# Four edits of order in a two-layer hybrid backbone: GLA's first projections, its scores and states, its gate products, and two adaLN k tiles

## The chip, the core and the metric

One core of a Trainium2 chip runs the whole program in one launch. The metric is device microseconds of that core, the median of several runs. TensorE (PE) multiplies, VectorE (DVE) and ScalarE (ACT) do elementwise work and empty PSUM, GpSimd (POOL) does a few small operations, SyncE (SP) issues every DMA.

## The reference, cut to what matters

Two layers work on 256 latent and 256 context tokens of width 1024. Each layer is: an adaLN-modulated RMS norm, one input projection, three token mixers, gated merging, an output projection with a gated residual, a second modulated norm, and a squared-ReLU MLP with a gated residual.

```python
sh1, sc1, ga1, sh2, sc2, ga2 = split(c_silu @ mod_w + mod_b, 6)        # per layer; the same for the context
h = rms_norm(x) * (1 + sc1) + sh1
y1 = rglru_branch(...)      # two directions: a*h + u scans over tokens, times gelu(y)
y2 = gla_branch(...)        # 4 heads, 2 directions: chunked gated linear attention, RMS norm, silu(r) gate
y3 = gqa_branch(...)        # 8 query heads, 2 key/value heads, softmax
x = x + ga1 * (merge of y1, y2, y3 by sigmoid gates) @ w_out
x = x + ga2 * squared_relu_mlp(rms_norm(x) * (1 + sc2) + sh2)
```

In GLA, with b the running sum of the log gates in a chunk of 64 tokens, a direction computes `scores = (q exp(b - b_mid)) (k exp(b_mid - b))^T`, masked, and a state `s` that decays by `exp(b_last)` from chunk to chunk and takes up `(k exp(b_last - b))^T v`. The output is `scores v + (q exp(b)) s`, summed over both directions.

## The kernel before, in words

Activations lie transposed: features on the partitions, the 512 tokens (context first, then latent) along the free axis. Layer 0 computes all tokens, layer 1 only the latent ones where the context isn't needed any more.

**Gemms.** `weight` (lines 191 to 202) loads a 512 KB tile of weights on SP's queue, casts it on ACT to a high part `wh` (L200) and subtracts on DVE for the low part `wl` (L201). `gemm` (line 252) makes 24 matmuls for 128 output features, `hi*hi`, `hi*lo` and `lo*hi` for each of eight k tiles, into one of the four PSUM banks of the pool `mm`. `gemm_tok` (line 265) does it token by token for four token tiles at once and wants four such banks. The other four banks are the pool `mx`. All matmuls of both helpers have the line L212.

**Order.** The program is traced as straight code. A scheduler then orders each engine's queue by priority, which is the place in the trace; `tc.high_priority(n)` moves a block n places ahead. It takes a lower instruction where the higher ones aren't ready, by its own estimate of time. The chip then runs each engine's queue in that order. Tiles come from pools with a fixed number of slots: `t2` has ten (`tmp()`), `g2` three (`gtmp()`), `t1` fifteen (`tmp1()`).

**RG-LRU and the passage to GLA.** Lines 605 to 622 go through eight channel tiles in pairs: convolution, gates on PE and ACT, decay, a square root (L614), then `lru_scan` (L529 to L540), ten DVE instructions and one cast on ACT (L282) for a tile. Behind the last pair's scans stand `gla_gates(0)`, the log gates of GLA's head 0 (Abs L585, Exp L588, Ln L589 on ACT; L586, L592 and two scans L594, L596 on DVE). Then `gla(0)` begins with the key and query gemms, copied out of PSUM on ACT by L637 and L640, and the value `gemm_tok`, copied by L645.

**A GLA head** (`gla`, line 632). For each direction: exponentials, scores on PE (L699, L701), a masked copy (L705), a turn of the decayed keys (L712) into `kt` (L715, L717, L718; from `t2`), and at once the three state products (L725) with their updates (L728, L730). Then the outputs (L744), their RMS norm (L746 to L751), and for each half j: the gate gemm, its silu (L755, L756; `y` from `t2`), the turn of the output (L759), their product and its split into two parts. Behind head 1 and head 2 stand four merges each (`merge`, line 767): two gemms, a tanh (L771) into a tile of `g2`, and a product into `m`.

**adaLN columns.** `mods` (line 310) is a task that is interleaved with the gemms by a clock of its own, which counts matmul columns: `tick` steps it when the clock has passed its next time. For each half of a unit (1024 columns) it loads eight k tiles of 256 KB. ACT makes the first product with the conditioning vector (L339) and DVE adds the others (L341), for two vectors. It pauses `pace` after each k tile and `M_S` at the end. `mod_cols` (line 288) then sums over the partitions on PE, by a matmul of each sum with a column of ones in `pick` (32 columns, one for each of four groups of PSUM partitions), and turns the row into columns of `modT` (L308). The turn of a half is traced behind the sum of the next one. Layer 0's second norm needs units 3 and 4: `need(l, 3, 4)` (line 953) steps the task until they are done.

Of the kernel before, what the change touches and what calls it, by code (L numbers as in the profile page):

```python
# [18 lines left out]
AF = mybir.ActivationFunctionType  # L19
# [4 lines left out]
KT = 8  # L24
# [13 lines left out]
GZP, G0P = 2, 6  # L38
AHEAD = 800
L_SM, L_PT = 4.0, 1.5  # L40
M_A, M_K, M_S = 300, 3.0, 2.0
NDVE = (0, 2, 5)
NL = 2
O_LX, O_LY, O_GQ, O_GK, O_GV, O_GR, O_GZ = 0, 1024, 2048, 2560, 3072, 4096, 5120
# [60 lines left out]
def trunk_kernel(ctx: ExitStack, tc: tile.TileContext, out: bass.AP, d: dict):  # L105
# [17 lines left out]
    def tmp():  # L123
        return t2.tile([128, 512], F32, name="t2")
# [163 lines left out]
    def mod_cols(l, n, terms, nk, dsts):  # L288

        ps = mx()  # L290
        for k in range(nk):
            w, r = terms(k)
            for j in range(4):
                mm(ps[32 * j:32 * j + 32, :n], w, r(n * j), start=k == 0, stop=k == nk - 1)
        sb = tmp1()
        S.copy(sb[:, :n], ps[:, :n])
        yield 0.0
        pt = mx()
        m = n // 128
        for i in range(m):  # L300
            tp(pt[:, 128 * i:128 * i + 128], sb[:, 128 * i:128 * i + 128])

        src = pt[:, :n].rearrange("p (i j b) -> p j i b", i=m, j=4)[:, :, :, 0:2]
        q = 4 // len(dsts)
        for h, o in enumerate(dsts):
            dst = modT[l][:, o:o + q * m, :].rearrange("p (j i) b -> p j i b", j=q)
            bia = pc(l, "modb", o, q * m).rearrange("p (j i) -> p j i", j=q).unsqueeze(3).to_broadcast([128, q, m, 2])
            V.tensor_tensor(dst, src[:, q * h:q * h + q], bia, op=ALU.add)  # L308

    def mods(l, us, pace):  # L310

        halves = [(u, j) for u in us for j in range(2)]

        def load(u, j, k):
            with tc.high_priority(M_A):
                t = tmp()
                nc.sync.dma_start(t, d["mod_w"][l, u][:, k, 512 * j:512 * j + 512])
            return t  # L320

        def turn():
            if last:
                for _ in last[0]:
                    pass
                if last[2]:
                    done.add((l, last[1]))

        last = None
        for u, j in halves:  # L330
            bs = (0, 1) if l == 0 or u < 2 else (1,)
            acc = [tmp() for _ in bs]
            nx = load(u, j, 0)
            for k in range(KT):
                t, nx = nx, load(u, j, k + 1) if k + 1 < KT else None
                for a, b in zip(acc, bs):
                    c = cs[:, k, b:b + 1]
                    if k == 0:
                        S.activation(a, t, AF.Copy, scale=c)  # L339
                    else:  # L340
                        V.scalar_tensor_tensor(a, t, c, a, op0=ALU.mult, op1=ALU.add)  # L341
                yield pace
            yield M_S
            g = mod_cols(l, 128, lambda i, acc=acc, bs=bs: (pick[:, bs[i], :], lambda c: acc[i][:, c:c + 128]),
                         len(bs), (4 * u if j == 0 else 8 + 4 * u,) if u < 2 else (8 * u + 4 * j,))
            next(g)
            turn()
            last = g, u, j
        yield pace
        turn()  # L350
# [110 lines left out]
    for l in range(NL):  # L461
# [22 lines left out]
        def gate_y(i):  # L484
            w = first[i] if l == 0 and i < 2 else weight(l, "in", O_LY + 128 * i, hi=E_LYH)
            ps = gemm(w, hh, hl, c0)
            ge[i] = x[:, i, :256] if last else tmp()
            S.activation(ge[i], ps, AF.Gelu_apprx_tanh)
# [82 lines left out]
        def gla_gates(h):  # L571
# [25 lines left out]
                bs.append(e)  # L597
            return bs

        LYS = LYS0, LYS1  # L600
        ly = iter(range(8))
        for j in range(LYS[l][0]):
# [2 lines left out]
        for i in range(0, 8, 2):  # L605
            lru_conv(i + 1)
            lru_gates(i)
            if i < 6:
                lru_conv(i + 2)
            lru_gates(i + 1)  # L610
            for j in range(2):
                lru_decay(i + j)
            tt = ws_[1][:, i % 4:i % 4 + 2]
            S.activation(tt, tt, AF.Sqrt, scale=0.25, bias=epsc)  # L614
            for j in range(LYS[l][i // 2 + 1]):
                gate_y(next(ly))
            for j in range(2):
                lru_scan(i + j)
            if i == GZP:
                zs = gla_z()  # L620
            if i == G0P:
                gates0 = gla_gates(0)


        hg = sm.tile([128, 2], F32, name="hg")
# [1 line left out]

        y2h, y2l = ytiles("yl")

        v2 = {}  # L630

        def gla(h):
            bs = gla_gates(h) if h else gates0

            pk = gemm(weight(l, "in", O_GK + 128 * h), hh, hl, 0)
            k_ = tmp()
            cp(E_K)(k_, pk)  # L637
            pq = gemm(weight(l, "in", O_GQ + 128 * h), hh, hl, c0)
            q_ = tmp()
            S.activation(q_[:, c0:], pq, AF.Copy, scale=128.0 ** -0.5)  # L640
            if h % 2 == 0:
                for t, ps in gemm_tok(l, O_GV + 256 * h, hh, hl, range(4)).items():
                    for a in range(2):
                        v2[h + a, t] = tmp1()
                        cp(E_V)(v2[h + a, t], ps[:, 256 * a:256 * a + 256])  # L645
            v_ = [v2.pop((h, t)) for t in range(4)]

            lo = c0 // 64
            nq = 8 - lo
            t0 = c0 // 128  # L650
            st = [[None] * 4 for _ in range(2)]
            pts, qhs = [], []
            for dd in range(2):
                b = c64(bs[dd])
                il, im = (63, 31) if dd == 0 else (0, 32)
# [54 lines left out]
                pkt = mx()  # L710
                for t in seq[:3]:
                    P.transpose(pkt[:, 128 * t:128 * t + 128], kh[:, 128 * t:128 * t + 128], ident)  # L712
                kt = tmp()
                if dd == 0:
                    cp(E_KT)(kt[:, :384], pkt[:, :384])  # L715
                else:
                    S.copy(kt[:, :256], pkt[:, :256])  # L717
                    S.copy(kt[:, 384:], pkt[:, 384:])  # L718
                cur = None
                for j, t in enumerate(seq):  # L720
                    st[dd][t] = cur
# [27 lines left out]
            for t in range(t0, 4):  # L749
                o = on[t - t0]  # L750
                V.tensor_scalar(o, o, rs[:, t:t + 1], None, op0=ALU.mult)  # L751
            for j in range(2):
                pr = gemm(weight(l, "in", O_GR + 256 * h + 128 * j), hh, hl, c0)
                y = tmp()
                S.activation(y[:, c0:], pr, AF.Tanh, scale=0.5)  # L755
                V.scalar_tensor_tensor(y[:, c0:], y[:, c0:], 1.0, pr, op0=ALU.add, op1=ALU.mult)  # L756
                po = mx()
                for t in range(t0, 4):
                    P.transpose(po[:, 128 * t:128 * t + 128], on[t - t0][:, 128 * j:128 * j + 128], ident)  # L759
                V.scalar_tensor_tensor(y[:, c0:], po[:, c0:], hg[:, j:j + 1], y[:, c0:],  # L760
                                       op0=ALU.mult, op1=ALU.mult)
                split_to(y2h[:, 2 * h + j, c0:], y2l[:, 2 * h + j, c0:], y[:, c0:])
# [142 lines left out]
        for st_ in QORD[l]:  # L905
            if st_ == "q":
                qs[len(qs)] = gqa_q(len(qs))
            elif st_ in "01":
                for g in ((0, 1), (2, 3)):
                    spawn(attend(int(st_), g, *qs[int(st_)]))  # L910
            elif st_ == "f":
                finish()
            elif st_ == "m":
                merge(1, next(mi), y2h, y2l)
            elif st_ == "u" and l == 0:
                spawn(mods(0, range(2, 6), M_K))
        if l:
            finish()
        mh, ml = ytiles("yh")
# [52 lines left out]
        for c in range(5):  # L972
            if c < 4:
                hid[c] = ytiles(("yh", "yl")[c % 2])
                n = NSPL if c == 0 and not last else 0
                for a, b in halves:
                    for i in range(n):
                        up(c, i, a, b)
                for i in range(n, 8):
                    up(c, i, c0, T)  # L980
            if c == 0:
                need(l, 5)
            if c == 4 and not last:
                need(1, 0, 1)
                hn1 = norm_mul(l + 1, 1)
                for a, b in halves[::-1]:
                    for i in range(8):
                        down(3, i, a, b)
                    with tc.high_priority(NHP):
                        norm_apply(l + 1, 1, x, a, b, norm_stats(x, a, b), hn1, range(8))  # L990
            elif c > 0:
                for i in range(8):
                    down(c - 1, i, c0, T)
                    if c == 4:
                        nc.sync.dma_start(out[:, i, :], x[:, i, 256:])
            if l == 0 and c == 0:
                spawn(mods(1, range(5), 1.5 * M_K))
        x1 = x


# [101 lines left out]
```

## Time and profile before

| what | value |
|---|---|
| median of 3 runs | 1927.91 us (1926.07 to 1928.13) |
| the profiled execution | 1926.13 us, its span 1924.3 us |
| PE busy | 1819.8 us (95%) |
| DVE busy | 1273.0 us (66%) |
| ACT busy | 926.4 us (48%) |
| PE's mean granted clock | 0.98 of full |

Times in the rows are microseconds from the span's start. `<-` behind an idle time names the engine, tile and line that ended it. Layer 0 runs to about 1200 us. In it, RG-LRU ends near 200, GLA near 455, the output gemms and the second norm lie at 763 to 860.

### The profile page before, as it was taken

To read this page: it belongs to the slowest core of one execution; us is meant where nothing else is said; L and a number is where in the kernel's file an instruction comes from. 1 tells how busy PE (TensorE), PEld (TensorE's weight loads), DVE (VectorE), ACT (ScalarE), POOL (GpSimd) and SP (SyncE) were. 2 spreads that over 40 slices of the span, in tenths; PEclk is the share of its full clock that TensorE was granted. 3 is DMA by queue.
4 is the path that set the end of the run, shared out by engine and by line. 5 is a ranking of instruction groups with operands and counts; after the bars stand their busy time and mean duration, and the time that the engine had idled before them with its cause. 6 is when DMAs were issued, how large, how long until landed. Compare 5 with 4: busy or idle time off the path is not lost.

```text
span 1924.3 us, 27716 instructions
## 1 busy us (share of the span) xinstructions
PE 1819.8 (95%) x10696; PEld 1544.4 (80%) x10696; DVE 1273.0 (66%) x2137; ACT 926.4 (48%) x1586; POOL 58.0 (3%) x88
## 2 busy tenths in 40 slices
PE   5998999999999999779999999996999999999999
PEld 4765778887777888778888889764888878999999
DVE  5677764445566984889854448787765677566665
ACT  3778544343443333454332325877654554445442
POOL 1000000000000000010000000000000000000000
PEclk9999999999999999879999999998999999999999
DMA  9322223222221653847643236531433333664654
GB/s 313 99 74 69 68 71 97 76 90 77 66 66 45 224 170 124 271 130 235 209 133 99 93 94 191 159 124 62 129 120 114 123 115 98 240 182 148 186 180 150
DMA packets 91619, 255.66 MB, mean 133 GB/s; under 512 B 9184, under 2 KB 20576, under 8 KB 91488
## 3 DMA queue, kind: packets, MB, share of 16 engines
q1 hardware_dynamic: 91488, 253.90, 41.6%
q8 instruction: 84, 1.38, 0.3%
q14 instruction: 47, 0.39, 0.1%
HBM read 252.82 MB, written 1.05 MB: 132 GB/s over the span
## 4 chain that ended last, share of the span: by engine, by line
PE 58%; issue 30%; DVE 6%; ACT 4%; POOL 1%; DMA 1%; SPq 0%; POOLq 0%; DVEq 0%; ACTq 0%
PE mm L212 49%; PE mx L212 2%; PE mx L744 1%; PE mx L725 1%; DVE wl L201 1%; ACT wh L200 1%; DVE t L341 1%; PE mx L216 1%; PE mx L699 1%; PE mx L510 1%; DMA t<-mod_w 1%; DVE lru L530 0%; PE mx L701 0%; DVE lru L529 0%; ACT lru L614 0%
## 5 line engine op out<-in xcount | busy, mean ns | idle before, releaser
L201 DVE TENSOR_TENSOR wl<-wraw,wh 128x1024 fp32r<-128x1024 f32 x365 | 445.9, 1224 | 297.7 <-ACT wh L200 294.5
L200 ACT CAST wh<-wraw 128x1024 fp32r<-128x1024 f32 x363 | 380.1, 1049 | 539.5 <-PE mm L212 464.2
L212 PE MATMUL mm<-hh,wh 128*128 128x512 f32 (+1 forms) x1448 | 500.3, 346 | 12.7 <-DVE big L933 6.1
L212 PE MATMUL mm<-hl,wh 128*128 128x512 f32 (+1 forms) x1448 | 496.4, 343 | 0.0
L212 PE MATMUL mm<-hh,wl 128*128 128x512 f32 (+1 forms) x1448 | 495.6, 342 | 0.0
L212 PEld LDWEIGHTS mm<-hh,wh 128*128 128x128 f32 x1448 | 276.3, 191 | 46.4 <-issue 9.6
L212 PEld LDWEIGHTS mm<-hl,wh 128*128 128x128 f32 x1448 | 276.0, 191 | 32.6 <-issue 3.5
L212 PEld LDWEIGHTS mm<-hh,wl 128*128 128x128 f32 x1448 | 275.8, 191 | 31.7 <-issue 1.4
L212 PE MATMUL mm<-yh,wh 128*128 128x512 f32 (+1 forms) x640 | 225.2, 352 | 3.3 <-DVE big L933 3.3
L212 PE MATMUL mm<-yh,wl 128*128 128x512 f32 (+1 forms) x640 | 225.0, 352 | 0.0
L212 PE MATMUL mm<-yl,wh 128*128 128x512 f32 (+1 forms) x640 | 223.3, 349 | 0.0
L212 PE MATMUL mm<-yp,wh 128*128 128x256 f32 x1024 | 190.6, 287 | 3.8 <-ACT g L771 2.3
L212 PEld LDWEIGHTS mm<-yp,wh 128*128 128x128 f32 x1024 | 161.1, 193 | 6.0 <-ACT g L771 2.5
L341 DVE SCALAR_TENSOR_TENSOR t<-t,cs,t 128x512 f32<-128x512 f32 x210 | 149.3, 752 | 12.7 <-DMA t<-mod_w 9.0
L212 PE MATMUL mm<-yp,wl 128*128 128x256 f32 x512 | 146.4, 286 | 0.8 <-DVE wl L201 0.8
L212 PEld LDWEIGHTS mm<-yh,wh 128*128 128x128 f32 x640 | 122.4, 191 | 18.7 <-DVE big L933 3.6
L212 PEld LDWEIGHTS mm<-yh,wl 128*128 128x128 f32 x640 | 122.1, 191 | 15.2 <-issue 0.5
L212 PEld LDWEIGHTS mm<-yl,wh 128*128 128x128 f32 x640 | 122.1, 191 | 14.9 <-issue 0.5
L212 PE MATMUL mm<-wh,hh 128*128 128x512 f32 x288 | 115.6, 401 | 18.5 <-ACT t L637 18.1
L212 PE MATMUL mm<-wl,hh 128*128 128x512 f32 x288 | 115.1, 400 | 2.3 <-DVE wl L201 2.3
L212 PE MATMUL mm<-wh,hl 128*128 128x512 f32 x288 | 114.4, 398 | 0.0
L933 DVE SCALAR_TENSOR_TENSOR big<-mm,modT,big 128x256 f32<-128x256 f32 x96 | 44.1, 481 | 89.0 <-PE mm L212 88.9
(223 smaller groups left out, 2223.9 us busy)
## 6 DMA issues: line engine op xcount, KB each, us to landing
wraw<-wt SPq DMA_DIRECT2D x365, 512.0 KB, 3.6
t<-mod_w SPq DMA_DIRECT2D x144, 256.0 KB, 3.9
modw<-mod_w SPq DMA_DIRECT2D x6, 2048.0 KB, 14.3
big<-xt SPq DMA_DIRECT2D x8, 512.0 KB, 5.2
gw<-lruw SPq DMA_DIRECT2D x16, 256.0 KB, 3.5
out<-big SPq DMA_DIRECT2D x8, 128.0 KB, 1.9
t<-glaw SPq DMA_DIRECT2D x8, 96.0 KB, 3.1
t<-ropeg SPq DMA_DIRECT2D x2, 256.0 KB, 2.7
```

Of the source, the lines that this page charges most:

```text
L200: S.copy(wh, r)
L201: (G if lo == "G" else V).tensor_tensor(wl, r, wh.bitcast(F32), op=ALU.subtract)
L212: P.matmul(o, a, b, **kw)
L216: P.transpose(o, a, ident)
L341: V.scalar_tensor_tensor(a, t, c, a, op0=ALU.mult, op1=ALU.add)
L510: P.matmul(pg, gw[:, 2 * dd + q, :], xc, start=True, stop=True)
L699: P.matmul(psc[:, c], en[:, c], em[:, c], start=True, stop=True)
L725: P.matmul(pu[:, :256], kt[:, 128 * t:128 * t + 128], v_[t], start=True, stop=True)
L744: P.matmul(po[:, :256], a, b, start=j == 0, stop=j == len(mm) - 1)
L933: V.scalar_tensor_tensor(x[:, i, c], ps[:, 256 * s - a:256 * s - a + 256], s0[:, i, s:s + 1], x[:, i, c], op0=ALU.mult, op1=ALU.add)
```

## The change

Order only, apart from the products of two k tiles, which move from DVE to PE:

- Ahead of the last two `lru_scan`s, `gla_gates(0)` and the new `gla_proj(0)` (the key, query and value projections of head 0, taken out of `gla`) are traced.
- In a head, the loop over directions ends at `kt`, which now comes from `g2`; a second loop does the states.
- Both gate gemms and their silus are traced ahead of both turns; `y` comes from `g2`.
- `mods` has a parameter `nd`: k tiles from `nd` on aren't multiplied on DVE, but go to `mod_cols` raw, as further terms with the conditioning vectors' columns `cs[:, k, :]` as weights. The call for units 2 to 5 of layer 0 takes `nd = 6` and a pace of 2.8 instead of 3.0. The call for layer 1 keeps its pace of 4.5 and all eight tiles on DVE.

```diff
-    def mods(l, us, pace):
+    def mods(l, us, pace, nd=KT):
...
             acc = [tmp() for _ in bs]
+            terms = [(pick[:, b, :], a) for a, b in zip(acc, bs)]
             nx = load(u, j, 0)
             for k in range(KT):
                 t, nx = nx, load(u, j, k + 1) if k + 1 < KT else None
+                if k >= nd:
+                    terms.append((cs[:, k, :], t))
+                    continue
...
-            g = mod_cols(l, 128, lambda i, acc=acc, bs=bs: (pick[:, bs[i], :], lambda c: acc[i][:, c:c + 128]),
-                         len(bs), (4 * u if j == 0 else 8 + 4 * u,) if u < 2 else (8 * u + 4 * j,))
+            g = mod_cols(l, 128, lambda i, terms=terms: (terms[i][0], lambda c: terms[i][1][:, c:c + 128]),
+                         len(terms), (4 * u if j == 0 else 8 + 4 * u,) if u < 2 else (8 * u + 4 * j,))
...
+        def gla_proj(h):
+
+            pk = gemm(weight(l, "in", O_GK + 128 * h), hh, hl, 0)
+            k_ = tmp()
+            cp(E_K)(k_, pk)
+            pq = gemm(weight(l, "in", O_GQ + 128 * h), hh, hl, c0)
+            q_ = tmp()
+            S.activation(q_[:, c0:], pq, AF.Copy, scale=128.0 ** -0.5)
+            if h % 2 == 0:
+                for t, ps in gemm_tok(l, O_GV + 256 * h, hh, hl, range(4)).items():
+                    for a in range(2):
+                        v2[h + a, t] = tmp1()
+                        cp(E_V)(v2[h + a, t], ps[:, 256 * a:256 * a + 256])
+            v_ = [v2.pop((h, t)) for t in range(4)]
+            return k_, q_, v_
...
+            if i == G0P:
+                first_head = gla_gates(0), gla_proj(0)
             for j in range(2):
                 lru_scan(i + j)
             if i == GZP:
                 zs = gla_z()
-            if i == G0P:
-                gates0 = gla_gates(0)
...
         def gla(h):
-            bs = gla_gates(h) if h else gates0
...
+            bs, (k_, q_, v_) = (gla_gates(h), gla_proj(h)) if h else first_head
...
-                kt = tmp()
+                kt = gtmp()
...
+                kts.append((kt, decp))
+            for dd, (kt, decp) in enumerate(kts):
+                seq = (0, 1, 2, 3) if dd == 0 else (1, 0, 3, 2)
                 cur = None
                 for j, t in enumerate(seq):
...
+            ys = []
             for j in range(2):
                 pr = gemm(weight(l, "in", O_GR + 256 * h + 128 * j), hh, hl, c0)
-                y = tmp()
+                y = gtmp()
                 S.activation(y[:, c0:], pr, AF.Tanh, scale=0.5)
                 V.scalar_tensor_tensor(y[:, c0:], y[:, c0:], 1.0, pr, op0=ALU.add, op1=ALU.mult)
+                ys.append(y)
+            for j, y in enumerate(ys):
                 po = mx()
...
-                spawn(mods(0, range(2, 6), M_K))
+                spawn(mods(0, range(2, 6), 2.8, KT - 2))
...
-                spawn(mods(1, range(5), 1.5 * M_K))
+                spawn(mods(1, range(5), 4.5))
```

## Rows read from the trace of the kernel before

**Rows 1.** The page, part 1: busy us, share of the span, instructions.

```profile
PE 1819.8 (95%) x10696; PEld 1544.4 (80%) x10696; DVE 1273.0 (66%) x2137; ACT 926.4 (48%) x1586; POOL 58.0 (3%) x88
```

**Rows 2.** Windows of 50 us: stretch, length, busy by engine, clock, DMA share, GB/s.

```profile
800.00:850.00 50.00, 26.94 (x204) 23.82 (x203) 45.65 (x85) 19.54 (x41) 5.67 (x7) 0.71 0.53 174
```

**Rows 3.** PE's timeline at layer 0's second norm: start, us, line, out<-in, count, idle before.

```profile
804.07 0.28 PE L212 MATMUL mm<-yh,wl 128*128 128x256 f32 x1
...
819.41 1.23 PE L212 MATMUL mx<-t,pick 128*32 128x128 f32 x16 [10.57 <-DVE t L341]
...
824.30 0.58 PE L212 MATMUL mm<-yh,wh 128*128 128x256 f32 x1 [3.27 <-DVE big L933]
824.68 0.41 PE L212 MATMUL mm<-yl,wh 128*128 128x256 f32 x1
...
843.92 0.55 PE L212 MATMUL mm<-hh,wh 128*128 128x256 f32 x1 [6.08 <-DVE big L933]
```

**Rows 4.** Timeline of ACT (first row) and DVE at the same place.

```profile
787.25 0.37 ACT L390 COPY t<-mx 128x256 f32<-128x256 f32 x1 [0.80 <-PE mx L388]
...
821.08 0.17 DVE L308 TENSOR_TENSOR modT<-mx,par 128x8 f32<-128x8 f32 x1 [0.16 <-PE mx L216]
...
827.51 0.75 DVE L283 TENSOR_TENSOR hl<-t,hh 128x256 fp32r<-128x256 f32 x2
```

**Rows 5.** Windows of the line L341 alone: stretch, DVE busy, clock, DMA, GB/s.

```profile
620.00:710.00 90.00, 48.45 (x70) 1.00 0.61 199
710.00:790.00 80.00, 0.00 (x0) 1.00 0.47 150
790.00:824.00 34.00, 21.49 (x30) 0.76 0.68 236
824.00:850.00 26.00, 8.53 (x12) 0.76 0.45 142
```

**Rows 6.** Timeline of SP's queue: loads of mod_w, the last and the next.

```profile
701.55 0.33 SPq L319 DMA_DIRECT2D t<-mod_w  x1
...
784.43 0.43 SPq L319 DMA_DIRECT2D t<-mod_w  x1
```

**Rows 7.** PE's timeline at the column products of one adaLN half.

```profile
694.59 0.64 PE L212 MATMUL mx<-t,pick 128*32 128x128 f32 x16
695.16 0.33 PE L216 MATMUL mx<-ident,t 128*128 128x128 f32 x1
```

**Rows 8.** PE's timeline in the value projection of head 0, both layers.

```profile
190.34 0.80 PE L212 MATMUL mm<-wh,hh 128*128 128x512 f32 x1 [7.65 <-ACT t L637]
190.94 0.63 PE L212 MATMUL mm<-wl,hh 128*128 128x512 f32 x1
...
1339.95 0.79 PE L212 MATMUL mm<-wh,hh 128*128 128x512 f32 x1 [10.42 <-ACT t L637]
```

**Rows 9.** ACT's timeline at the same places.

```profile
185.59 1.06 ACT L589 ACTIVATE eb<-eb 128x1024 f32<-128x1024 f32 x1
...
189.71 0.58 ACT L637 COPY t<-mm 128x512 f32<-128x512 f32 x1
...
1335.95 1.06 ACT L589 ACTIVATE eb<-eb 128x1024 f32<-128x1024 f32 x1
...
1339.32 0.58 ACT L637 COPY t<-mm 128x512 f32<-128x512 f32 x1
```

**Rows 10.** PE's waits in GLA, layer 0 and layer 1: total us, times, longest.

```profile
PE mx L759 <- DVE t L751: 3.8, 4, 0.9
...
PE mx L759 <- DVE t L751: 2.3, 4, 0.8
```

**Rows 11.** Timeline of ACT and PE in head 1 of layer 1.

```profile
1397.39 0.38 ACT L771 ACTIVATE g<-mm 128x256 f32<-128x256 f32 x1
...
1397.82 0.39 PE L212 MATMUL mm<-yp,wh 128*128 128x256 f32 x1 [2.28 <-ACT g L771]
...
1412.63 0.68 ACT L755 ACTIVATE t<-mm 128x256 f32<-128x256 f32 x2
```

More of the change, by code (lines that the diff above doesn't have):

```diff
@@ L40 @@
 L_SM, L_PT = 4.0, 1.5
-M_A, M_K, M_S = 300, 3.0, 2.0
+M_A, M_S = 300, 2.0
 NDVE = (0, 2, 5)
@@ L598, in gla_gates @@
             return bs
+        v2 = {}
+        def gla_proj(h):
[12 more added lines that the diff above has]
+            return k_, q_, v_
         LYS = LYS0, LYS1
@@ L628, in trunk_kernel @@
         y2h, y2l = ytiles("yl")
-        v2 = {}
         def gla(h):
-            bs = gla_gates(h) if h else gates0
[L635 to L646, printed above, removed]
+            bs, (k_, q_, v_) = (gla_gates(h), gla_proj(h)) if h else first_head
             lo = c0 // 64
@@ L651, in gla @@
             st = [[None] * 4 for _ in range(2)]
-            pts, qhs = [], []
+            pts, qhs, kts = [], [], []
             for dd in range(2):
```

## The prediction

> **What bounds the kernel now.** I read the page's engine table first: PE is busy for 1819.8 of 1924.3 us [rows 1], so the most that a new order can win is the 104.5 us in which PE stands, and what it loses at the lower clock behind each stand. The windows of 50 us then show where that lies: in most windows PE is busy for 47 us or more, from 800 to 850 us for only 26.94, at a mean granted clock of 0.71, while DVE has 45.65 [rows 2]. The reader is to see that this is the largest hole behind the start-up. Other engines count only where PE waits for them, so the third view is PE's timeline, hole by hole.
>
> The profiled execution took 1926.1 us (span 1924.3 and 1.8 around it). The sum is made against that; the three timed runs have their median 1.8 us higher, and less than 0.2% (about 4 us) can't be told from no change.
>
> **Edit 1: two raw k tiles in the late adaLN halves of layer 0.** PE runs out of work at 804, waits up to 10.57 us at a time for DVE's L341, and comes back at 824.30 with 0.41 us for a matmul that took 0.28 before; at 843.92 it waits 6.08 us again, for a residual on DVE [rows 3]. In 800 to 850 it stands for 50 - 26.94 = 23.1 us [rows 2]. The cause is the need(l, 3, 4) ahead of the second norm. The statistics of the context half are in SBUF at 787.6, and the last modT column comes only at 821.08 [rows 4]. DVE did 70 of the L341 steps up to 710, none in the next 80 us, and 30 more in 790 to 824 [rows 5]. SP shows why: the loads of mod_w stop at 701.55 and start again at 784.43 [rows 6]. I counted the loads that the code has traced when it reads need(l, 3, 4), by adding the matmul columns in its own clock: 8 output gemms behind 11 merges are 133 us of that clock, a half costs eight steps of 3.2 (3.0 rounded up to the 0.64 of one k of a gemm), 2.6 for the pause and 1.8 of its own: five halves, 40 loads. SP issued exactly 40 up to 701.55. The others are traced behind the norm's own tiles of the same pool t2, so they wait for these.
>
> After the change a half has six paced steps (2.8 also rounds up to 3.2), 2.6, and 3.5 of its own: 25 instead of 30. By the same count seven halves, all that u = 3 and 4 need (the columns of a half are turned one half later), are traced before need(l, 3, 4), the last by the eighth output gemm. DVE has 10 steps for a half instead of 14; eight halves save 32 of about 0.7 us (21.49 / 30) [rows 5], which is cover and not path. So modT should be there at about 787, with the statistics, and not at 821. Norm_apply took 7 us from modT to its last split [rows 4]; PE has output gemms of the latent half until about 807 (804, and the last one of 2.9 us that now waits; 24 matmuls at 0.12 us). The stand should nearly go: -23.1. The clock: 0.76 over 824 to 850 means about 12.5 us at the lower of the two levels, 6.1 of them idle [rows 3, 5]; the 6.4 us of work there, and some 2 behind 850, would take half: -4. What is late next is the norm of the latent half: statistics and then another 7 us of norm_apply behind its last residual, with five `up` gemms of 2.9 us beside them, close enough that I leave 3 us of waiting: +3.
>
> Added is PE work: a half has four terms instead of two. Two terms take from 694.59 to 695.16, 0.57 us [rows 7]; eight halves give +4.6. The Trainium skill, TensorE: Matmul & The Clock Gate, Part 3, says that matmuls in different column groups run side by side, about 4 ns apart. By that rule the sum for this term would be about +2.2 (an estimate: 16 terms of two passes of some 68 ns). The trace agrees only in part: the 16 records stand 36 ns apart, less than one takes alone and far more than 4.
>
> A raw tile holds its t2 slot until PE uses it, so a half holds 4 of the 10 slots and DVE can run two halves ahead, not five: 50 us of PE time, where a half's loads and steps took 74 / 5 = 15 us. Loads are not more, and are spread over 155 us instead of 74; SP's queue, in which the weights stand behind them, gets less dense. Edit 1 in all: -23.1 - 4 + 3 + 4.6 = -19.5. Bounds: -25 with no waiting left and cheap terms, -8 if only the 10.57 goes.
>
> **Edit 2: GLA's first projections ahead of the last scans.** PE stands 7.65 us at 190.34 and 10.42 us at 1339.95, in the value projection of head 0, for the key copy L637, and then has some matmuls of 0.63 us [rows 8]. Key and query stand in two of the four mm banks, so the value gemm, which wants four, can't go on. On ACT, L637 starts at 189.71 and 1339.32, behind the cast of a scan's result, though the Ln before it ends at 186.65 and 1337.01 [rows 9]. With the new order L637 is traced ahead of both scans. Its t2 tile is traced behind those of the gates' L586 on DVE, which now also go ahead. But the square root and the gates' Abs, Exp and Ln stay ahead of it on ACT, without a gap; so I let it start when the Ln ends: 3.1 us earlier in layer 0 and 2.3 in layer 1. The scans' ten DVE steps for an i are put behind the gates' six (about 5 us); nothing of PE waits for the scans until the first merge, 60 us on. The weight casts that waited behind the scans' casts come earlier too; for that I add 0.6. Edit 2: -6. Bounds: 0 (another instruction takes the place) to -21 (both stalls and their slow matmuls go: 18.1 + 3).
>
> **Edit 3: both gate products, then turns.** PE waits at the eight L759 turns for 3.8 us in layer 0 and 2.3 in layer 1 [rows 10]. It could now run what is left of the second gate gemm there; in heads 0 and 2 of layer 0 something was left (two waits of 0.95), in the others it had been done. -2, from 0 to -6.1.
>
> **Edit 4: scores of both directions, then states; kt and y from g2.** The two state updates that leave the second direction's way are short (0.47 us each on DVE), and the total stays. The pool is what changes: g2 has three slots, and now holds two kt and two y of each head beside the merges' g. In layer 1 the first merge of head 1 ran ahead of the head's states: its tanh is at 1397.39, the head's own gate tanh at 1412.63, and in between PE, after 2.28 us for that tanh, did the 48 matmuls of the next merge [rows 11]. With the pool served in the order of tracing, that g comes behind kt and y; all four mm banks (two gate products, two of the merge) are then full from 1395 to 1413, and 48 x 0.127 = 6.1 us of filler are pushed out. At the other heads that have merges their tanh comes behind the gates' already. Against it, t2 has four tiles of a head fewer, which may free about 1 us of the waits for L637. +5, from -3 to +9.
>
> **Sum.** -19.5 - 6 - 2 + 5 = -22.5: 1926.1 - 22.5 = 1903.6, say 1904. All lower ends together would be 1871, all upper ends 1927.
>
> **Rivals.**
> A: the second wait takes the place of the first. The latent half's norm isn't covered by the five `up` gemms, since DVE still has eight L341 steps there and stood in front of the residual before (6.08 us). For it: DVE's 45.65 in that window. Against: 24 fewer steps there. Edit 1 would give about -10: 1913.
> B: the key copy finds a gap on ACT as soon as the gates' tiles are there, and both stalls go whole. For it: ACT was idle for some microseconds ahead of the last gates. Against: that gap lies before the gates. Another -13: 1891.
> C, slower: the raw tiles starve the halves. A half's loads can start only when PE has turned the half two before; if SP's loads then come late, PE, in order, stands at each of the eight column products. It decides when a half's loads and steps take longer than the 22 to 25 us that PE gives it. The longest wait of a load for a column product is about 4 us now; 4 us at each of eight is 32: 1936. Against: 15 us for a half now.
> D: the change doesn't do what it says: DVE or the pool keeps modT late, and the small edits cancel: 1924 to 1930.
>
> **How the numbers follow.** Forecast 0.62 (its own range 1896 to 1910), A 0.17, B 0.12, D 0.04, C 0.05. Forecast, A and B are all faster by over 0.2%: 0.91; D is within it: 0.04; C is slower: 0.05. Leaving out C, D and the outer parts of A and B, the range is 1888 to 1916.
>
> **What would show it.** Right: PE busy for over 45 us in the window that holds the second norm of layer 0, modT's last column within 3 us of the statistics, 112 - 32 = 80 L341 steps in layer 0; L637 directly behind the Ln, with stalls of about 4.5 and 8 us; a new PE wait of several us at head 1 of layer 1, for g or y. Wrong: PE waiting at the column products (C), a wait of over 8 us for a residual or hl (A), no wait for L637 at all (B), or mod_w loads that still have a gap of tens of us.

## The result and the profile after

The changed kernel takes 1904.4 us (median of 4 runs, 1899.9 to 1905.4) against 1927.7 before: ratio 0.9876, 95% interval 0.9859 to 0.9893. The forecast was 1904. The profiled execution of after is the shortest of its four (span 1898.1), so times below are compared between points of one trace, and gains by the ratios of timed runs.

Lines have moved: L345 is the former L341 (column step), L610 the key copy L637, L593 the Ln L589, L705 the scores L699, L771 the turns L759, L783 the merge's tanh L771, L765 the gate product's tanh L755, L945 the residual L933. In the runs further down they lie up to three lines off these.

The engine table of after, which answers to [rows 1]:

```profile
PE 1817.9 (96%) x10824; PEld 1545.2 (81%) x10824; DVE 1252.0 (66%) x2105; ACT 924.9 (49%) x1586; POOL 60.8 (3%) x88
```

PE's busy time is the same to 2 us, with 128 more matmuls, and the span is 26 us shorter: nearly all that went is standing time. The windows of 50 us answer to [rows 2] (stretch, length, busy by engine, granted clock, DMA share, GB/s):

```profile
780.00:830.00 50.00, 45.60 (x392) 43.84 (x391) 42.60 (x84) 30.79 (x60) 7.59 (x10) 1.00 0.57 181
800.00:850.00 50.00, 45.76 (x369) 42.94 (x368) 42.50 (x78) 30.15 (x58) 3.71 (x5) 1.00 0.65 216
```

The hole at the second norm of layer 0 is gone: PE 45.76 in place of 26.94, at a granted clock of 1.00 (2.4 GHz) in place of a mean of 0.71. The windows of the line L345 alone answer to [rows 5]:

```profile
620.00:710.00 90.00, 35.07 (x50) 1.00 0.65 203
710.00:790.00 80.00, 17.08 (x24) 1.00 0.65 204
790.00:824.00 34.00, 4.38 (x6) 1.00 0.59 192
```

That is the 80 steps of layer 0, and 24 of them now lie where before there were none. The reason is in SP's queue, to be read against [rows 6]; DVE's rows below it are the last column that the norm needs and the statistics it is applied with, for [rows 4]:

```profile
749.67 0.33 SPq L319 DMA_DIRECT2D t<-mod_w  x1
759.36 0.35 SPq L319 DMA_DIRECT2D t<-mod_w  x1
791.92 1.66 SPq L319 DMA_DIRECT2D t<-mod_w  x3
```

```profile
780.93 0.16 DVE L308 TENSOR_TENSOR modT<-mx,par 128x8 f32<-128x8 f32 x1
785.91 0.16 DVE L135 TENSOR_SCALAR rs<-mx 128x2 f32<-128x2 f32 x1 [0.76 <-PE mx L385]
```

The same statistics instruction in the kernel before:

```profile
785.13 0.16 DVE L135 TENSOR_SCALAR rs<-mx 128x2 f32<-128x2 f32 x1 [0.76 <-PE mx L381]
```

There still is a gap in the loads, from 759 to 792, but it comes after 59 of them in place of 40, and all that `need(l, 3, 4)` asks for lies ahead of it. modT is complete 5 us before the statistics; in the kernel before it came at 821.08, 36 us behind the same instruction.

The value projection of head 0, for [rows 8] (PE; the figure in brackets is how long it stood) and [rows 9] (ACT):

```profile
185.71 0.50 PE L212 MATMUL mm<-wh,hh 128*128 128x512 f32 x1 [2.10 <-ACT t L610]
...
209.85 1.16 PE L705 MATMUL mx<-t,t 128*128 128x128 f32 x8 [2.60 <-DVE t L699]
...
1309.34 0.80 PE L212 MATMUL mm<-wh,hh 128*128 128x512 f32 x1 [5.63 <-ACT t L610]
...
1332.68 0.71 PE L705 MATMUL mx<-t,t 128*128 128x128 f32 x4 [2.78 <-DVE t L699]
```

```profile
184.13 1.06 ACT L592 ACTIVATE eb<-eb 128x1024 f32<-128x1024 f32 x1
185.09 0.57 ACT L610 COPY t<-mm 128x512 f32<-128x512 f32 x1
185.67 1.28 ACT L593 ACT_TABLE_LOAD   x1
186.97 1.06 ACT L593 ACTIVATE eb<-eb 128x1024 f32<-128x1024 f32 x1
```

The key copy stands between Exp and Ln, not behind the Ln. The stalls for it fell from 7.65 to 2.10 and from 10.42 to 5.63 us; behind them there are new ones of 2.60 and 2.78 at head 0's first scores, whose operands DVE prepares beside the last scans.

In head 1 of layer 1, ACT and PE now read, against [rows 11]:

```profile
1378.12 0.37 ACT L723 COPY g<-mx 128x256 f32<-128x256 f32 x1 [3.42 <-PE mx L718]
...
1378.54 0.41 ACT L765 ACTIVATE g<-mm 128x256 f32<-128x256 f32 x1
...
1381.76 0.38 ACT L783 ACTIVATE g<-mm 128x256 f32<-128x256 f32 x1 [0.79 <-PE mx L734]
```

```profile
1375.41 1.22 PE L705 MATMUL mx<-t,t 128*128 128x128 f32 x4 [3.51 <-DVE t L699]
```

The first merge's tanh (L783) was 15 us ahead of the head's own gate tanh, and is now 3 us behind it.

### The profile page after: what moved, and what is told of

Its sections match the earlier page's. It is cut to its first block, busy times and chain, and to the rows that moved or that the text cites. A ratio compares the mean times of both kernels' runs of the same rounds, so it can differ in the third digit from the quotient of the medians.

```text
span 1898.1 us, 27875 instructions
## 1 busy us (share of the span) xinstructions
PE 1817.9 (96%) x10824; PEld 1545.2 (81%) x10824; DVE 1252.0 (66%) x2105; ACT 924.9 (49%) x1586; POOL 60.8 (3%) x88
## 4 chain that ended last, share of the span: by engine, by line
PE 39%; issue 11%; DVE 4%; ACT 4%; POOL 1%; DMA 0%; SPq 0%; POOLq 0%; DVEq 0%; ACTq 0%
PE mm L212 35%; PE mx L212 1%; DVE wl L201 1%; ACT wh L200 1%; PE mx L514 1%; PE mx L734 1%; PE mx L753 0%; ACT lru L636 0%; DVE lru L534 0%; ACT lru L515 0%; DVE lru L533 0%; ACT lru L526 0%; ACT lru L519 0%; PE mx L216 0%; POOL t L413 0%
## 5 line engine op out<-in xcount | busy, mean ns | idle before, releaser
L345 DVE SCALAR_TENSOR_TENSOR t<-t,cs,t 128x512 f32<-128x512 f32 x178 | 127.3, 746 | 32.7 <-DMA t<-mod_w 22.3
L212 PEld LDWEIGHTS mm<-yp,wl 128*128 128x128 f32 x512 | 98.7, 193 | 1.1 <-issue 1.0
```

Source lines behind the costliest of these rows:

```text
L212: P.matmul(o, a, b, **kw)
```

## Experiments

A gain in us below is the ratio less one, times the 1926 us of before. The first four kernels ran on one chip with the same runs of before, and so did the next four and the last four.

**One edit alone on the kernel before, I.** Of the diff above only `mods` and its two calls:

```diff
-                spawn(mods(0, range(2, 6), M_K))
+                spawn(mods(0, range(2, 6), 2.8, KT - 2))
```

> Only the first edit (two raw adaLN k tiles in layer 0's steps, pace 2.8), on the kernel before. Theory (this edit carries the gain): the traces of before and after stand 21.2 us apart over its stretch, so 1906 to 1908, and the wait at the second norm of layer 0 is gone. Rival (the edits of the GLA heads share the gain, and the later stretch only moved with them): 1912 to 1920.

Measured: 1905.8, ratio 0.9893 (0.9879 to 0.9906): -20.6 us (-23.3 to -18.1). Edit 1 carries nearly the whole gain.

**Pace alone.** Does the place of the loads count, or the VectorE work saved?

```diff
-                spawn(mods(0, range(2, 6), M_K))
+                spawn(mods(0, range(2, 6), 1.9))
```

> The kernel before with one number changed: the pace of the steps in layer 0 is 1.9 instead of 3.0, no raw tile, all 112 later column steps kept on VectorE. By the clock of the code all seven halves that the norm needs are then traced before it (64 loads instead of 40). Theory (what counted is the place of the loads in the order of tracing): the hole goes as with the raw tiles, and the extra matmuls (predicted at 4.6 us) are saved too: 1901 to 1906. Rival (what counted is the VectorE work that the raw tiles take away, 32 of 112 steps): the norm still waits for the chain of steps, or attention's softmax waits behind them: 1915 to 1930.

Measured: 1898.6, ratio 0.9857 (0.9844 to 0.9871): -27.5 us, below the whole changed kernel, by one number and with all 112 column steps kept on VectorE. It came out lower than either theory had it. The column steps' windows and the norm's window in its trace:

```profile
620.00:710.00 90.00, 49.58 (x72) 1.00 0.65 214
710.00:790.00 80.00, 27.63 (x40) 1.00 0.64 205
```

```profile
800.00:850.00 50.00, 48.88 (x373) 46.84 (x372) 42.81 (x76) 31.96 (x60) 3.64 (x5) 1.00 0.74 227
```

All 112 steps are done by 790, with no raw tile, and PE is busy for 48.88 of the 50 us. VectorE had room for them all along (none in the 80 us from 710 in [rows 5]); what it lacked was loads. Against the raw tiles alone the pace saves 7.2 us by medians. Some 3.5 of them are the extra products (worked out below), and PE's waits on DVE from 750 to 870 are 2.1 us in this trace and 6.3 in that one; why they differ stays open.

**Raw tiles at a late pace.** The same question from the other side:

```diff
-                spawn(mods(0, range(2, 6), 2.8, KT - 2))
+                spawn(mods(0, range(2, 6), 4.8, KT - 2))
```

> The first edit alone with the pace at 4.8 instead of 2.8, so that 38 loads instead of 59 are traced before the norm (40 in the kernel before). Theory (place in the order of tracing): the hole at the norm stays, only shorter by the VectorE steps that are forced there (22 instead of 28, some 4 us): 1922 to 1930. Rival (the VectorE work saved): most of the gain stays, 1906 to 1913.

Measured: 1930.7, ratio 1.0023 (1.0014 to 1.0032): slower than before by 4.4 us, with the same 32 steps taken off VectorE as in edit 1. The rival falls. SP's queue and PE at the norm:

```profile
740.80 0.86 SPq L319 DMA_DIRECT2D t<-mod_w  x2
788.47 0.42 SPq L319 DMA_DIRECT2D t<-mod_w  x1
```

```profile
811.21 0.62 PE L212 MATMUL mx<-t,cs 128*32 128x128 f32 x16
821.68 1.22 PE L212 MATMUL mx<-t,pick 128*32 128x128 f32 x16 [5.96 <-DVE t L345]
822.68 1.08 PE L212 MATMUL mx<-t,cs 128*32 128x128 f32 x16
```

The loads stop and come back at the norm as before, and PE stands for L345 again. The 0.7 us over the theory's range are a miss of mine. PE's standing time fell by 3.4 us as I had thought (1928.8 - 1827.7 = 101.1, before 104.5), but its busy time rose by 7.9 (1827.7, before 1819.8), which the range had not counted. The raw terms are in that, part of them in the slow stretch behind the stand (granted clock 0.50 from 821.68 to 823.68); how much else is in it was not taken apart, and PE's busy time differs by some us between traces even with equal matmuls (1825.2 for edit 2 alone).

**One edit alone, II.** Gates and first projections of head 0 ahead of the last scans:

```diff
+            if i == G0P:
+                first_head = gla_gates(0), gla_proj(0)
             for j in range(2):
                 lru_scan(i + j)
...
-            if i == G0P:
-                gates0 = gla_gates(0)
```

> Only the second edit (gates and first projections of head 0 ahead of the last scans), on the kernel before. Theory (the key copy now comes between Exp and Ln on ScalarE): the stalls in the value projection fall from 7.65 and 10.42 us to 2.1 and 5.6, less the new waits of 2.6 and 2.8 us at the first scores: 1927.7 - 10.3 + 5.4 to 1927.7 - 9.5, that is 1918 to 1923. Rival (the gain in the GLA stretches came from the other edits): 1925 to 1929.

Measured: 1920.5, ratio 0.9968 (0.9959 to 0.9977): -6.2 us (-7.9 to -4.4). Its trace has the stalls of after at the value projection (2.11 and 5.62) and new ones at the first scores (1.54 and 2.93).

**One edit alone, IV.** Scores of both directions, then states, kt and y from the pool g2:

```diff
-                kt = tmp()
+                kt = gtmp()
...
+                kts.append((kt, decp))
+            for dd, (kt, decp) in enumerate(kts):
...
-                y = tmp()
+                y = gtmp()
```

> Only the fourth edit (both directions' scores, then both directions' states, with kt and y in the pool of three tiles), on the kernel before. Theory (the tanh output of the first merges in layer 1's head 1 now comes behind kt and y in that pool, so that their matmuls no longer fill the head's waits): +4 to +6, so 1930 to 1933. Rival (that cost needs the other edits, or there is none): 1924 to 1928.

Measured: 1929.1, ratio 1.0022 (1.0013 to 1.0031): +4.2 us (2.5 to 6.0). The median is just below the theory's range in us (the runs of before beside it were lower), the ratio is inside it. PE and ACT in head 1 of layer 1:

```profile
1403.62 1.19 PE L707 MATMUL mx<-t,t 128*128 128x128 f32 x4 [5.64 <-DVE t L702]
1408.73 1.22 PE L707 MATMUL mx<-t,t 128*128 128x128 f32 x4 [2.46 <-DVE t L702]
```

```profile
1411.71 0.27 ACT L726 COPY g<-mx 128x128 f32<-128x128 f32 x1
1411.87 0.40 ACT L766 ACTIVATE g<-mm 128x256 f32<-128x256 f32 x1
...
1415.54 0.38 ACT L782 ACTIVATE g<-mm 128x256 f32<-128x256 f32 x1 [0.90 <-PE mx L736]
```

PE stands 8.1 us for score operands from DVE, in the place where it had done a merge; the merge's tanh (L782) comes behind the second kt copy (L726) and both gate tanhs.

**A tile of its own for the merge's tanh output**, in the changed kernel (layer 1, first branch):

```diff
+    gm = ctx.enter_context(tc.tile_pool(name="gm", bufs=1))
...
+            if last and b == 0:
+                g1 = gm.tile([128, 256], F32, name="gm")
+                S.activation(g1, pg, AF.Tanh, scale=0.5)
+                V.scalar_tensor_tensor(m[:, i, :], g1, 1.0, pb, op0=ALU.add, op1=ALU.mult)
+                return
```

> The changed kernel with one thing else: the tanh output of layer 1's first-branch merges has a tile of its own (one of 256 columns) and no longer shares the pool of kt and y. Theory (place in that pool's order): the merges fill head 1's waits again, and 3 to 5 us of the changed kernel's 1904.4 go: 1899 to 1901.5. Rival (the order of scores and states itself costs, or one tile in place of three holds the merges up): 1903.5 to 1908.

Measured: 1897.0, ratio 0.9844 (0.9829 to 0.9860), some 6 us below after by the ratios, with intervals that just touch, and lower than expected. ACT and PE:

```profile
1372.53 0.37 ACT L785 ACTIVATE gm<-mm 128x256 f32<-128x256 f32 x1
...
1382.41 0.40 ACT L766 ACTIVATE g<-mm 128x256 f32<-128x256 f32 x1
```

```profile
1374.94 0.87 PE L719 MATMUL mx<-ident,t 128*128 128x128 f32 x3 [0.33 <-DVE t L683]
1375.46 0.78 PE L213 MATMUL mm<-yp,wh 128*128 128x256 f32 x2
...
1380.49 0.61 PE L706 MATMUL mx<-t,t 128*128 128x128 f32 x4
```

The tanh is 10 us ahead of the gates again, and the next merge's matmuls run from 1375.46 to 1380.49, where after stood for 3.51 us.

**Changed kernel without edit 4** (edits 1 to 3; kt and y from the pool of ten, states inside the loop over directions):

```diff
-                kt = gtmp()
+                kt = tmp()
...
-                kts.append((kt, decp))
-            for dd, (kt, decp) in enumerate(kts):
```

> The changed kernel without its fourth edit: per direction scores, then states, as before; kt and y from the pool of ten. Theory (edit 4 costs 4 to 6 us): 1898 to 1901. Rival (it costs nothing, and the GLA stretch of layer 1 gives time back for another reason, such as head 0's scores beside the last scans): 1903 to 1906.

Measured: 1900.4, ratio 0.9867 (0.9852 to 0.9883). By medians 4.0 us below after, by ratios 1.7, and the intervals overlap: in this setting the price of edit 4 is between nothing and some 5 us.

**Pace 1.9 in place of the raw tiles, with edits 2 and 3, without edit 4**:

```diff
-                spawn(mods(0, range(2, 6), 2.8, KT - 2))
+                spawn(mods(0, range(2, 6), 1.9))
```

> Edits 2 and 3 with the pace of 1.9 in place of the raw tiles, and without edit 4. Theory (the parts add: -28 for the pace, -6.1 for edit 2 as each measured alone, -1 for edit 3): 1890 to 1894. Rival (the second norm's hole and the GLA heads overlap in what they gain, or the later column steps collide with edit 3): 1896 to 1900.

Measured: 1892.0, ratio 0.9826 (0.9813 to 0.9840): the parts add.

**All four edits, pace 1.9 and the own tile** (the two diffs above together):

> All four edits, with the pace of 1.9 in place of the raw tiles and the own tile for the tanh output of layer 1's first-branch merges. Theory (the parts add: 1897.0 with the own tile, less the 7.2 that lie between the pace alone and the raw tiles alone): 1888 to 1892. Rival (the column steps left on VectorE collide with the new order in the GLA heads): 1893 to 1897.

Measured: 1889.7 (1886.3 to 1891.1), ratio 0.9813 (0.9800 to 0.9827). This is below both kernels: 35.6 us under the runs of before beside it, 14.7 under after's median.

**Own tile without edit 4**: edits 1 to 3 with the own tile, as in the diffs shown.

> Edits 1 to 3, without edit 4, and with the own tile for the merges' tanh output. Theory (the tile only undoes a conflict that edit 4 brings, and here is none): 1899 to 1902, as without the tile; then the 3.4 us between that kernel and the one with edit 4 and the tile are what the order of scores and states itself is worth. Rival (the tile helps any order): 1895 to 1898.

Measured: 1900.0, ratio 0.9870 (0.9857 to 0.9884), as without the tile. So the tile gains only where edit 4 had put other tiles in the way. With the tile, the kernel with edit 4 is lower by 3.0 us of medians (0.26 points of ratio, intervals that just touch): the new order itself may be worth some microseconds, which the pool had eaten, but that is not shown.

**y back in the pool of ten**, kt left in the pool of three, in the changed kernel:

```diff
-                y = gtmp()
+                y = tmp()
```

> The changed kernel with the gate product's y back in the pool of ten; kt stays in the pool of three. Theory (y is what stands ahead: with kt, kt and then the first merge's tanh output in three tiles, that merge starts early again): 1897 to 1900. Rival (kt alone holds the merges back, or y now waits in the pool of ten): 1903 to 1908.

Measured: 1901.5, ratio 0.9878 (0.9865 to 0.9892). The time lies between the two ranges; by the ratio it is the same as after (0.9876) and clear of the kernel with the own tile (0.9844, up to 0.9860). My theory on y fell. ACT there, in head 1 of layer 1:

```profile
1379.55 0.27 ACT L724 COPY g<-mx 128x128 f32<-128x128 f32 x1
1380.40 0.39 ACT L765 ACTIVATE t<-mm 128x256 f32<-128x256 f32 x1
1380.68 0.39 ACT L783 ACTIVATE g<-mm 128x256 f32<-128x256 f32 x1
```

Three tiles would hold two kt and the merge's g, and yet the merge's tanh comes only behind the second kt copy. ACT stood for 1.97 us before 1377.83 and 1.07 us before 1379.28 and did not take it. So it isn't the number of tiles. The rows fit a pool that gives its tiles out in the order of tracing: kt of the second direction is traced ahead of g and made late.

**One edit alone, III.** Both gate products, then both turns:

```diff
+                ys.append(y)
+            for j, y in enumerate(ys):
```

> Only the third edit (both gate products, then both turns), on the kernel before. Theory (only one of eight short waits goes, as in the trace of after): -0.5 to -1.5, so 1924.5 to 1926.5. Rival (all eight waits go when the edit stands alone, as the upper bound of the prediction had it): 1920 to 1922.

Measured: 1923.1, ratio 0.9994 (0.9985 to 1.0003), -1.2 us (-2.9 to +0.6): not told from no change, and between the two ranges. PE's turn waits in its trace, layer 0 and layer 1:

```profile
PE mx L770 <- DVE t L759: 1.9, 2, 1.0
...
PE mx L770 <- DVE t L759: 2.3, 4, 0.8
```

Alone, the edit removes two of the eight waits, those of heads 0 and 2 in layer 0, and not one as my theory had it.

## Why the prediction was right

The total (-22.5 forecast, -23.9 by the ratio) isn't right by luck of large errors: each edit alone came out near its own forecast, though edit 2 by luck. The four edits alone have ratios whose product is 0.9893 x 0.9968 x 0.9994 x 1.0022 = 0.9877, the whole change 0.9876.

| step | forecast us | alone, us (95%) |
|---|---|---|
| edit 1 | -19.5 | -20.6 (-23.3 to -18.1) |
| edit 2 | -6 | -6.2 (-7.9 to -4.4) |
| edit 3 | -2 | -1.2 (-2.9 to +0.6) |
| edit 4 | +5 | +4.2 (+2.5 to +6.0) |

- **Edit 1, mechanism: shown.** Moving the loads ahead of the norm's tiles without raw tiles brings the gain (pace alone), and raw tiles with the loads left behind bring none (late pace). The saved VectorE steps bring no net gain here: PE stood 3.4 us less, but the kernel was slower.
- **Edit 1, terms.** The stretch that the edit touches is taken from four turns on PE (L216, 631.59 before) to a table load on ACT early in layer 1 (1214.10 before), the same two instructions in each trace. Its windows, for before, after and the pace alone (length, PE busy):

```profile
631.59:1214.10 582.51, 558.10 (x3130) 478.66 (x3129) 403.70 (x616) 225.72 (x344) 15.55 (x20) 0.97 0.51 164
626.85:1188.19 561.34, 555.76 (x3258) 476.83 (x3257) 382.73 (x584) 223.62 (x344) 14.85 (x20) 1.00 0.55 170
631.72:1188.06 556.34, 552.59 (x3128) 474.31 (x3127) 402.75 (x616) 224.56 (x345) 14.50 (x20) 1.00 0.55 172
```

  It is 21.2 us shorter in after, for a forecast of 19.5. PE stands 5.6 us in place of 24.4, that is 18.8 less (forecast -23.1 + 3 = -20.1). PE's busy time lost 5.5 us with the pace alone, which adds no products; I take that for the clock, whose mean there goes from 0.97 to 1.00 (forecast 4). The products were sized too high, at 4.6. Four terms of a half take from 674.61 to 675.62 in after, 1.01 us, where two took 0.57, so the two added ones cost 0.44, or 3.5 us for eight halves; by the windows it is 3.2.

```profile
674.61 0.64 PE L212 MATMUL mx<-t,pick 128*32 128x128 f32 x16
675.07 0.62 PE L212 MATMUL mx<-t,cs 128*32 128x128 f32 x16
675.62 0.33 PE L216 MATMUL mx<-ident,t 128*128 128x128 f32 x1
```

  So the three errors are of 1 to 1.5 us and partly cancel. The 3 us left for what is late next are 4.1 in after (PE's waits from 785 to 860):

```profile
PE mm L212 <- DVE big L945: 2.8, 1, 2.8
PE mm L212 <- DVE g L978: 0.8, 1, 0.8
PE mx L392 <- DVE t L391: 0.5, 1, 0.5
```

  The rule cited from the Trainium skill, TensorE: Matmul & The Clock Gate, Part 3 (matmuls in different column groups start some 4 ns apart), gave +2.2 as an estimate for this term; the measured 3.5 lies between it and the forecast. The trace doesn't show 4 ns: the first 16 records take 0.46 us from start to start, 29 ns each.
- **Edit 2: the sum right, two of its steps wrong.** The step "I let it start when the Ln ends" failed: the copy comes behind the Exp, and the stalls lost 5.55 and 4.79 us in place of 3.1 and 2.3. The step "nothing of PE waits for the scans until the first merge" failed too: the scores' operands share DVE with the scans, and PE waits 2.60 and 2.78 for them in after. 10.3 less 5.4 is 4.9 (in the edit alone 10.3 less 4.5 is 5.9), near the forecast of 6 by luck: the copy's earlier start gave 5 us more than forecast, and the scores' waits took as much away.
- **Edit 3: the waits right alone, less so in the whole.** The two waits that the prediction named, in heads 0 and 2 of layer 0, are the ones that went in the edit alone (its time is not told from no change). In after PE waits 2.8 us (3 times) and 2.5 (4 times) at the turns, 5.3 of 6.1 in [rows 10]; only head 2's wait of layer 0 went:

```profile
PE mx L771 <- DVE t L760: 2.8, 3, 1.0
...
PE mx L771 <- DVE t L760: 2.5, 4, 0.7
```

- **Edit 4: place and size right, the chain only in part.** The filler was pushed out in head 1 of layer 1, but kt alone is enough for it, and PE then waits for score operands, not for g or y as the signs to look for had it.
- **Still open.** The worth of the new order of scores and states by itself (3.0 us by medians, with intervals that touch), and the price of edit 4 inside the whole change (1.7 us by ratios, 4.2 alone); kt in the pool of ten together with the new order was not tried.
- **Signs.** PE's window (45.76), the 80 steps and the stall at head 1 of layer 1 came as named. modT was 5 us ahead of the statistics, where "within 3" was named. L610 is not behind the Ln but ahead of it. One sign of being wrong is there as well: the loads of mod_w still have a gap of 32 us (759 to 792). It was a bad sign: only five loads lie behind the gap, all of the eighth half, which the norm doesn't need.
- **Rivals.** A (a second wait in place of the first) would show over 8 us for the residual; it is 2.8. B (no wait for the key copy) is refuted by 2.10 and 5.63. C (PE starved at the column products) has no wait there in after. D fell with the time.

## What to carry to other kernels

Where a pool's tiles are given out in the order of tracing, an early producer traced late is a late producer: count what is traced ahead of the point that needs it before taking work off an engine, and try moving the tracing first. Here one number of pace gained more than the raw tiles did. A tile that feeds filler work needs a pool in which nothing traced before it is made later. Two edits of one change can have opposite signs; time each alone.

## What was not expected of the hardware

A second pair of column terms right behind a first costs less than the pair alone: 0.44 us against 0.57, as told above. Behind a stand of 5.96 us column terms cost about twice as much: sixteen records took 1.22 us at 821.68 of the late-pace kernel, where the granted clock is 0.50 (1.2 GHz), and 0.64 at 674.61 of after, where it is 1.00. ScalarE took a copy of 0.57 us between the Exp and the table load of the Ln; in the trace of before the two stand back to back (the Exp at 183.22 for 1.06 us, the load at 184.30).
